# Router stage of a hybrid encoder block: GpSimd's elementwise work on VectorE, the affinities sorted in four partition groups, TensorE in program order, token-layout weights at another offset

## The chip, the core and the metric

The kernel runs on one core of a Trainium2 chip. The metric is the device time in microseconds of one execution, taken as the median of several runs. The engines named below: TensorE (PE; its weight loads are PEld), VectorE (DVE), ScalarE (ACT), GpSimd (POOL), and SyncE (SP), which issues DMAs.

## What is computed

One layer of an encoder block on 1024 tokens of width 1024, in float32: windowed attention and a gated linear attention (GLA) side by side, an output projection added to x, then an expert-choice mixture of 16 SwiGLU experts, then a gate with per-layer embeddings and a last norm. The change is in the router stage between the output projection and the experts, and in the weights of the first projections. Cut to these:

```python
a = rmsnorm(h, norm_mix[l])
proj = a @ w_in[l]            # q, k, v, q_gla, k_gla, v_gla, r_gla, z, gates
...
h = h + merged @ w_out[l]
xn = rmsnorm(h, norm_ffn[l])
aff = softmax(xn @ w_router)                          # 1024 tokens x 16 experts
top_aff, top_idx = top_k(swapaxes(aff, 1, 2), 128)    # each expert takes 128 tokens
xg = xn[top_idx]
hid = silu(xg @ w_gate) * (xg @ w_up)
y = (hid @ w_down) * top_aff                          # added back at top_idx
...
h = h + sigmoid(rmsnorm(h) @ w_pg) * (p[l] @ w_ple)
```

## The kernel before

Every float32 operand of a large product is split into a rounded upper part and a lower part that holds the rest (`split`: a cast on ScalarE, a subtraction on VectorE or on the engine named), and a product is three matmuls in a row (`mm3`, lines 109 to 111). The 1024 tokens are eight tiles of 128.

**The first projections.** `piece` (line 196) loads a column block of w_in of 8 x 128 rows and 256 columns and splits it into wh and wl. In `proj_tok` such a weight is the moving operand, 128x256, and a block of the transposed activations aT (128x128) the stationary one; the result has tokens on its partitions. This "token layout" is used for k and v (w_kv, 8 tiles x 8 blocks x 3 matmuls = 192), for q (two pieces, 384) and for GLA's v (one piece a head, 768). In `proj_T`, for the rest, the weight is stationary. Tiles come from pools whose tiles are whole lines of 128 bytes (`Lines`); those of wh and wl lie in the pool whl (4 buffers), q's second piece in wqp.

**The router stage.** The loop over tiles t calls `w_half(t, c, between)` for both halves c of the 1024 output columns: 8 blocks k of three 128x512 matmuls each into one bank, and then, on VectorE, the sum ht = 0.5 * bank + x (line 995). At the start of tile t the next tile's input is split by `msplit` (lower part on GpSimd from tile 1 on). After the second half, ScalarE squares ht and VectorE makes 1/rms of it (`rstd_of`, lines 113 to 136, some ten instructions of 128x1). The dictionary `between` says before which block k a step of the tile before is called:

- `h_turned`: eight transposes of ht into two banks "tr", copied to hT by ScalarE
- `router`: eight small matmuls of hT with the router's weights; logits copied by ScalarE
- `affinities`: a transpose back, then the softmax over 16 experts (VectorE, ScalarE) into affA
- `aff_turned`: affA of the tile transposed to 16 experts x 128 tokens, copied by ScalarE into cand; the row xa (ht times the norm's gain, on GpSimd, with affinities and 1/rms behind it) goes to DRAM for the gather

The four steps stand at k = 2, 4, 6 of half 0 and k = 2 of half 1. After tile 2 the weights w_ple are split (lower part on GpSimd); after tile 5 `p_turned` turns the embeddings p through the two banks "tr" and splits them.

**The sort.** Each expert needs its 128 largest affinities. `top128` takes eight maxima a round (MAX8) and strikes them out (MATCH_REPLACE8): on 16 partitions, 256 candidates wide, for tiles 0 and 1, 2 and 3, 4 and 5, 16 rounds each; `merge` joins two sorted lists by a bitonic net (`larger`, then seven stages of max and min). Tiles 6 and 7 are sorted at the end in halves of 64. Then the threshold cg, the masks, the positions of the chosen tokens (`tokens`) and the gather of the first expert's rows follow.

**What sets the order.** A scheduler orders each engine's instructions from the dependencies and its own estimates of time; it may put an instruction ahead of one that is written earlier. Only in the expert stage are TensorE's instructions tied to program order (`on_pe`). The product p @ w_ple (`p_product`) is written behind the gather; the scheduler puts it in the tail, between the last projection and the gather.

## Time and profile before

| | |
|---|---|
| median of 3 runs | 1739.63 us (1738.83 to 1740.87) |
| the profiled execution's own time | 1741.5 us |
| its span, first to last instruction | 1739.8 us |
| mean granted TensorE clock | 0.983 |
| busy: TensorE, VectorE, ScalarE, GpSimd | 1658.0, 1201.4, 902.2, 196.4 us |
| router stage (tile 1 to the end of the projection) | 894 to 1010 us |
| its tail (to the first expert's matmul) | 1010 to 1048 us |

The busy time of an engine is what its instructions took; a stretch's granted clock is a share of TensorE's full 2.4 GHz, and 0.5 is its other level, 1.2 GHz. Engines wait for each other by semaphores; the profile names for each wait the instruction that ended it.

### The profile page before, as it was taken

To read this page: it belongs to the slowest core of one execution; us is meant where nothing else is said; L and a number is where in the kernel's file an instruction comes from. 1 tells how busy PE (TensorE), PEld (TensorE's weight loads), DVE (VectorE), ACT (ScalarE), POOL (GpSimd) and SP (SyncE) were. 2 spreads that over 40 slices of the span, in tenths; PEclk is the share of its full clock that TensorE was granted. 3 is DMA by queue.
4 is the path that set the end of the run, shared out by engine and by line. 5 is a ranking of instruction groups with operands and counts; after the bars stand their busy time and mean duration, and the time that the engine had idled before them with its cause. 6 is when DMAs were issued, how large, how long until landed. Compare 5 with 4: busy or idle time off the path is not lost. (4 is left out here: it accounts for less than half of the span.)

```text
span 1739.8 us, 23112 instructions
## 1 busy us (share of the span) xinstructions
PE 1658.0 (95%) x8795; PEld 1361.8 (78%) x8795; DVE 1201.4 (69%) x2256; ACT 902.2 (52%) x1259; POOL 196.4 (11%) x197
## 2 busy tenths in 40 slices
PE   7998999999999999999998859999999999999897
PEld 6977766768888888988876647888888887787786
DVE  7546765543464646473367898999999998888676
ACT  4235555352444444351032236777777777777642
POOL 1013300000000000000034320111111111000010
PEclk9999999999999999999998889999999999999999
DMA  6032401415121212027442379999999999993811
GB/s 231 2 105 110 133 13 61 133 61 194 39 84 37 84 38 72 14 102 237 143 174 98 120 295 408 371 393 393 385 398 394 395 384 373 377 376 97 283 49 49
DMA packets 123607, 335.06 MB, mean 193 GB/s; under 512 B 9180, under 2 KB 41988, under 8 KB 123496
## 3 DMA queue, kind: packets, MB, share of 16 engines
q1 hardware_dynamic: 106784, 277.96, 43.6%
q0 software_dynamic: 14704, 53.17, 9.0%
q10 hardware_dynamic: 2008, 2.46, 0.4%
q8 instruction: 69, 1.13, 0.3%
q14 instruction: 42, 0.34, 0.1%
HBM read 290.50 MB, written 43.06 MB: 192 GB/s over the span
## 5 line engine op out<-in xcount | busy, mean ns | idle before, releaser
L106 DVE TENSOR_TENSOR slot<-slot 128x2048 fp32r<-128x2048 f32 (+1 forms) x193 | 438.0, 2283 | 52.7 <-ACT slot L106 50.2
L106 ACT CAST slot<-slot 128x2048 fp32r<-128x2048 f32 (+1 forms) x200 | 374.9, 1879 | 129.9 <-PE ps_mm L1195 50.8
L109 PE MATMUL ps_mm<-aT_h,wh 128*128 128x512 f32 x512 | 203.3, 397 | 1.2 <-ACT sgr L246 1.2
L111 PE MATMUL ps_mm<-aT_h,wl 128*128 128x512 f32 x512 | 204.4, 399 | 0.0
L110 PE MATMUL ps_mm<-aT_l,wh 128*128 128x512 f32 x512 | 203.9, 398 | 0.0
L109 PEld LDWEIGHTS ps_mm<-aT_h,wh 128*128 128x128 f32 x512 | 97.3, 190 | 18.8 <-ACT sgr L246 1.4
L111 PEld LDWEIGHTS ps_mm<-aT_h,wl 128*128 128x128 f32 x512 | 97.5, 190 | 18.4 <-issue 1.2
L110 PEld LDWEIGHTS ps_mm<-aT_l,wh 128*128 128x128 f32 x512 | 97.3, 190 | 18.5 <-issue 1.2
L106 DVE TENSOR_TENSOR wl<-raw,wh 128x2048 fp32r<-128x2048 f32 (+1 forms) x29 | 61.5, 2121 | 65.0 <-ACT wh L106 65.0
L1195 PE MATMUL ps_b<-slot,xt_h 128*128 128x512 f32 x256 | 100.1, 391 | 4.0 <-DVE slot L106 4.0
L1195 PE MATMUL ps_mm<-slot,xt_h 128*128 128x512 f32 x256 | 100.2, 392 | 2.7 <-DVE slot L106 2.7
L1194 PE MATMUL ps_mm<-slot,xt_h 128*128 128x512 f32 x256 | 101.5, 396 | 0.5 <-ACT xt_h L106 0.5
L1194 PE MATMUL ps_b<-slot,xt_h 128*128 128x512 f32 x256 | 101.0, 395 | 0.0
L1196 PE MATMUL ps_mm<-slot,xt_l 128*128 128x512 f32 x256 | 100.1, 391 | 0.5 <-DVE xt_l L106 0.5
L106 ACT CAST wh<-raw 128x2048 fp32r<-128x2048 f32 (+1 forms) x30 | 52.0, 1734 | 93.4 <-PE ps_mm L110 89.1
L1196 PE MATMUL ps_b<-slot,xt_l 128*128 128x512 f32 x256 | 99.8, 390 | 0.0
L109 PE MATMUL ps_mm<-wh,aT_h 128*128 128x256 f32 x320 | 91.8, 287 | 0.9 <-DVE sgr L588 0.9
L111 PE MATMUL ps_mm<-wh,aT_l 128*128 128x256 f32 x320 | 90.6, 283 | 1.5 <-DVE aT_l L106 1.5
L110 PE MATMUL ps_mm<-wl,aT_h 128*128 128x256 f32 x320 | 90.8, 284 | 0.0
L109 PE MATMUL ps_mm<-slot 128*128 128x512 f32 x192 | 79.9, 416 | 0.0
L111 PE MATMUL ps_mm<-slot 128*128 128x512 f32 x192 | 77.8, 405 | 0.0
L110 PE MATMUL ps_mm<-slot 128*128 128x512 f32 x192 | 77.6, 404 | 0.0
(392 smaller groups left out, 3893.5 us busy)
## 6 DMA issues: line engine op xcount, KB each, us to landing
slot<-in_w_exp_gate_dram SPq DMA_DIRECT2D x64, 1024.0 KB, 7.7
slot<-in_w_exp_down_dram SPq DMA_DIRECT2D x64, 1024.0 KB, 8.1
slot<-in_w_exp_up_dram SPq DMA_DIRECT2D x60, 1024.0 KB, 7.6
raw<-in_w_in_dram SPq DMA_DIRECT2D x16, 1024.0 KB, 6.5
raw<-in_w_in_dram SPq DMA_DIRECT2D x14, 512.0 KB, 5.2
sg_d<-sgr POOLq DMA_DIRECT2D x14, 512.0 KB, 3.0
xn_d<-xa POOLq DMA_DIRECT2D x8, 520.5 KB, 4.3
xt<-in_x_dram SPq DMA_DIRECT2D x8, 512.0 KB, 6.6
```

Of the source, the lines that this page charges most:

```text
L106: return nc.scalar.copy(hi, src), eng.tensor_sub(lo, src, hi)
L109: nc.tensor.matmul(out_ps, sh, mh, start=start, stop=False)
L110: nc.tensor.matmul(out_ps, sh, ml, start=False, stop=False)
L111: nc.tensor.matmul(out_ps, sl, mh, start=False, stop=stop)
L1194: on_pe(nc.tensor.matmul(po[c], src[0][:, kk], hi[:, k, cc], start=first, stop=False))
L1195: on_pe(nc.tensor.matmul(po[c], src[0][:, kk], lo[:, k, cc], start=False, stop=False))
L1196: on_pe(nc.tensor.matmul(po[c], src[1][:, kk], hi[:, k, cc], start=False, stop=last))
```

## The change

1. **Token-layout weights.** `Lines` and `pool` take `behind`: the tiles of whl and wqp become 256 bytes longer, and a tile may begin some bytes behind its line. w_kv, w_q's first piece and the heads' w_v begin 192 bytes behind, w_q's second piece 64. In the built programs these operands begin, counted in units of 256 bytes, at 128 before (w_q's second piece at 0) and at 64 afterwards, all of them; the stationary aT at 128 in both.
2. **GpSimd.** The lower parts of `msplit` and of w_ple and the product xa are made by VectorE. GpSimd keeps the two small copies into xa, its DMA issues and five memsets.
3. **The sort.** The affinities of a tile go to 16 partitions in one of four groups (from partition 0, 32, 64, 96), so that one MAX8 serves up to four lists. Tiles 0 to 3 are sorted at once behind tile 3's turn (two halves of 64, eight rounds each), 4 and 5 behind tile 5's (each in two groups of 64 candidates), 6 and 7 each alone (four groups of 32, four rounds). Lists in different groups are copied side by side (`beside`) and joined or merged. Nothing is sorted before tile 3's turn.
4. **Order.** All matmuls and transposes go through `matmul` and `turn`, and from the router loop to the end of the experts TensorE is in program order. The steps stand at other places: `h_turned` at k = 3 and `router` at k = 6 of half 0, `affinities` at k = 1 and `aff_turned` at k = 7 (k = 3 for t = 6, 7) of half 1. Behind the last tile the p product is cut in eight pieces of six matmuls, written between the last tile's steps.
5. The token numbers of all experts lie in one tile, idxs.

```diff
-    def tile(self, shape, dt, **kw):
+    def tile(self, shape, dt, behind=0, **kw):
         n = math.prod(shape[1:])
+        if self.behind:
+            at = behind // SIZE[dt]
+            t = self.pool.tile([shape[0], n + self.behind // SIZE[dt]], dt, **kw)[:, at:at + n]
+            return self.shaped(t, shape)
...
+    def on_pe(ins):
+        if in_order[0]:
+            if behind[0] is not None:
+                tc.add_manual_dep(ins.ins, behind[0].name, ..., reason="program order")
+            behind[0] = ins.ins
+        return ins
...
-    whl = ctx.enter_context(pool("whl", bufs=4))
+    TOK = 192
+    whl = ctx.enter_context(pool("whl", bufs=4, behind=256))
...
-        w_v = piece([(0, w_in[:, C_VG + h * 256:C_VG + (h + 1) * 256])])
+        w_v = piece([(0, w_in[:, C_VG + h * 256:C_VG + (h + 1) * 256])], behind=TOK)
...
+    def sorted_tiles(t):
+        c = cand[t]
+        n = 128 // cut[t]
+        if n == 128:
+            for i in range(2):
+                largest(c[:, i * 64:i * 64 + 64], part[:, i * 64:i * 64 + 64], 64)
+            return joined(b1, part[:, 0:64], part[:, 64:128], b2)
+        largest(c, part[:, 0:n], n)
+        beside(part, n, ((0, 1), (2, 3)))
+        return joined(b1[0:80, 0:2 * n], part[0:80, 0:n], other[0:80, 0:n], b2[0:80, 0:2 * n])
...
+    def four_tiles():
+        s = sorted_tiles(0)
+        beside(s, 128, ((0, 1), (2, 3)))
+        s = merged(s[0:80], other[0:80], slice(0, 80), b2)
+        beside(s, 128, ((0, 2),))
+        merged(s[0:NE], other[0:NE], slice(0, NE), top)
+
+    def two_tiles():
+        s = sorted_tiles(4)
+        beside(s, 128, ((0, 2),))
+        s = merged(s[0:NE], other[0:NE], slice(0, NE), b2)
+        merged(top[0:NE], s, slice(0, NE), top)
+
+    def one_tile(t):
+        s = sorted_tiles(t)
+        beside(s, 64, ((0, 2),))
+        return joined(cand[0][0:NE], s[0:NE, 0:64], other[0:NE, 0:64], top2[0:NE])
...
-        split(hl[:, 0], hl[:, 1], mT[t // 2][:, :, t % 2 * 128:t % 2 * 128 + 128], nc.gpsimd if t else nc.vector)
+        split(hl[:, 0], hl[:, 1], mT[t // 2][:, :, t % 2 * 128:t % 2 * 128 + 128])
...
-        nc.gpsimd.tensor_mul(xa[:, 0:D], hts[t], nffn)
+        nc.vector.tensor_mul(xa[:, 0:D], hts[t], nffn)
...
-        if t == 2:
-            top128(cand[0], top[0], 256)
-        elif t in (4, 6):
-            top128(cand[t - 2], srt, 256)
-            merge(srt)
+        if t == 3:
+            four_tiles()
+        elif t == 5:
+            two_tiles()
+        elif t == 6:
+            merged(top[0:NE], one_tile(6), slice(0, NE), top)
...
-        before = [partial(f, t - 1) for f in steps] if t else []
-        w_half(t, 0, dict(zip((2, 4, 6), before)))
-        w_half(t, 1, dict(zip((2,), before[3:])))
+        was = [{}, {}]
+        if t:
+            was = [{3: partial(h_turned, t - 1), 6: partial(router, t - 1)},
+                   {1: partial(affinities, t - 1), (3 if t > 5 else 7): partial(aff_turned, t - 1)}]
+        for c in range(2):
+            w_half(t, c, was[c])
...
+    p_half(0)
+    for f, more in ((h_turned, (1,)), (router, (2,)), (affinities, (3, 4)), (aff_turned, (5, 6, 7))):
+        f(NT - 1)
+        for n in more:
+            p_half(n)
+    last = one_tile(NT - 1)
```

What it moves, at three places. In these rows a line number is that of the kernel they are from; slot stands for several buffers, ps_mm, ps_tr, ps_a and ps_b for banks.

**VectorE at the first sort.** Before, the sort of tiles 0 and 1 is written behind tile 2's turn, but the scheduler starts it in tile 2's projection, two tiles of candidates wide, and the sum of that tile's second half (SCALAR_TENSOR_TENSOR ht<-ps_mm) stands among its first rounds:

```order
L916 MAX top_8463<-cand_8458 16x8
L918 MATCH_REPLACE cand_8458<-top_8463,cand_8458 16x256
L916 MAX top_8463<-cand_8458 16x8
L995 SCALAR_TENSOR_TENSOR ht<-ps_mm,ht 128x512
L918 MATCH_REPLACE cand_8458<-top_8463,cand_8458 16x256
L916 MAX top_8463<-cand_8458 16x8
L918 MATCH_REPLACE cand_8458<-top_8463,cand_8458 16x256
L916 MAX top_8463<-cand_8458 16x8
L120 TENSOR_SCALAR rs_v_8767<-ss 128x1
L918 MATCH_REPLACE cand_8458<-top_8463,cand_8458 16x256
```

Now the sort of four tiles starts in tile 4's second half, and the sum of that half stands behind the last of its 16 MAX, ahead of the joins:

```order
L947 MATCH_REPLACE cand_8458<-part,cand_8458 128x64 x2
L945 MAX part<-cand_8458 128x8 x2
L947 MATCH_REPLACE cand_8458<-part,cand_8458 128x64 x2
L945 MAX part<-cand_8458 128x8 x2
L1063 SCALAR_TENSOR_TENSOR ht<-ps_mm,ht 128x512
L969 TENSOR_TENSOR b_8463<-part 128x64
L970 TENSOR_TENSOR b_8463<-part 128x64
L131 TENSOR_TENSOR slot<-slot 128x1024
L959 TENSOR_TENSOR b_8464<-b_8463 128x2x32
L960 TENSOR_TENSOR b_8464<-b_8463 128x2x32
L144 TENSOR_SCALAR rs_v_9094<-ss 128x1
L1123 TENSOR_TENSOR xa<-ht,nffn 128x1024
```

The sum moved from behind the fifth of 16 rounds to behind the last of 16, and a split and xa (128x1024) stand behind it.

**TensorE around the turn of the affinities.** Before, in tile 3's loop, the turn of tile 2's affinities (16x128) stands between the three matmuls of a product:

```order
L111 MATMUL ps_mm<-slot 128x512
L109 MATMUL ps_mm<-slot 128x512
L1045 MATMUL ps_a<-ident,affA 16x128
L110 MATMUL ps_mm<-slot 128x512
L111 MATMUL ps_mm<-slot 128x512
L109 MATMUL ps_mm<-slot 128x512
L110 MATMUL ps_mm<-slot 128x512
```

Now, from tile 4's loop into tile 5's: the transposes of the logits, the turn of tile 3's affinities, and the turn of tile 4's ht:

```order
L127 MATMUL ps_a<-ident,lg_8958 128x128
L124 MATMUL ps_mm<-slot 128x512 x18
L127 MATMUL ps_a<-ident,affA 16x128
L124 MATMUL ps_mm<-slot 128x512 x12
L127 MATMUL ps_tr<-ident,ht 128x128 x8
L124 MATMUL ps_mm<-slot 128x512 x9
```

Between the turn of the affinities, which starts the sort, and the turn of ht, which needs the sum behind the sort, now stand 12 matmuls.

**TensorE in the tail.** Before, the scheduler has put the last tile's steps among the matmuls of the p product (ps_b):

```order
L1010 MATMUL ps_tr<-ident,ht 128x128 x4
L109 MATMUL ps_b<-slot 128x512
L110 MATMUL ps_b<-slot 128x512
L111 MATMUL ps_b<-slot 128x512
L1010 MATMUL ps_tr<-ident,ht 128x128 x4
L1021 MATMUL ps_a<-hT,wr 32x128 x4
L109 MATMUL ps_b<-slot 128x512
L110 MATMUL ps_b<-slot 128x512
L111 MATMUL ps_b<-slot 128x512
L109 MATMUL ps_b<-slot 128x512
L1021 MATMUL ps_a<-hT,wr 32x128 x4
L110 MATMUL ps_b<-slot 128x512
```

Now they are in the order of the program, the p product in pieces between them:

```order
L124 MATMUL ps_mm<-slot 128x512 x15
L124 MATMUL ps_b<-slot 128x512 x6
L127 MATMUL ps_tr<-ident,ht 128x128 x8
L124 MATMUL ps_b<-slot 128x512 x6
L124 MATMUL ps_a<-hT,wr 32x128 x8
L124 MATMUL ps_b<-slot 128x512 x6
L127 MATMUL ps_a<-ident,lg_9630 128x128
L124 MATMUL ps_b<-slot 128x512 x12
L127 MATMUL ps_a<-ident,affA 16x128
L124 MATMUL ps_b<-slot 128x512 x18
L127 MATMUL ps_a<-ident,cg 128x16 x2
```

The turn of the last affinities (16x128) has 30 matmuls of the p product ahead of it, and 18 behind.

## Rows read from the trace of the kernel before

**Rows 1.** The table of stretches of core 0, by stage: the router stage, its tail, and the part of the expert stage that follows. Columns: the stretch, its length, busy us (and instructions) of TensorE's matmuls, its weight loads, VectorE, ScalarE and GpSimd, the granted TensorE clock as a share of full speed, the busy share of the DMA engines, GB/s.

```profile
894.00:1010.00 116.00, 100.41 (x532) 77.24 (x530) 90.74 (x292) 28.84 (x64) 45.96 (x42) 0.91 0.34 124
1010.00:1048.00 38.00, 17.60 (x106) 12.72 (x104) 31.57 (x163) 13.64 (x20) 8.93 (x9) 0.75 0.83 318
1048.00:1435.00 387.00, 385.46 (x1861) 317.72 (x1861) 354.93 (x224) 300.53 (x233) 53.45 (x23) 1.00 1.02 391
```

**Rows 2.** The same table for the stretches of the router stage in which the clock was granted at half; columns as in rows 1.

```profile
921.40:926.30 4.90, 4.86 (x12) 3.82 (x13) 4.42 (x14) 0.26 (x1) 0.75 (x2) 0.50 0.26 109
940.00:943.40 3.40, 3.40 (x10) 2.66 (x9) 1.87 (x7) 0.00 (x0) 0.00 (x0) 0.50 0.39 157
...
970.70:974.10 3.40, 3.40 (x10) 2.64 (x9) 3.13 (x14) 0.00 (x0) 0.00 (x0) 0.50 0.38 157
...
981.00:987.80 6.80, 4.44 (x20) 2.83 (x20) 4.07 (x16) 1.17 (x2) 0.85 (x2) 0.50 0.43 151
```

**Rows 3.** The waits of TensorE from 894 to 1048 us: what it waited for and on which engine; us in total, times, the longest.

```profile
PE ps_a L1045 <- DVE affA L1039: 11.0, 6, 5.1
PE ps_a L1092 <- DVE cg L1087: 7.8, 1, 7.8
...
PE ps_tr L1010 <- DVE slot L106: 4.6, 1, 4.6
```

**Rows 4.** The timeline of VectorE while tile 2 is projected, from the 1/rms of tile 1 to the first rounds of the sort: start in us, duration in us, engine, line, operation, out<-in, shapes, and in brackets the idle time before it with what ended it.

```profile
910.77 7.80 DVE L133 SCALAR_TENSOR_TENSOR rs_y<-rs_t,rs_y 128x1 f32<-128x1 f32 x1
...
918.92 0.16 DVE L133 SCALAR_TENSOR_TENSOR rs_y<-rs_t,rs_y 128x1 f32<-128x1 f32 x1
...
922.14 0.42 DVE L916 MAX8 top<-cand 16x8 f32<-16x256 f32 x1 [0.21 <-ACT cand L1046]
...
923.10 0.42 DVE L916 MAX8 top<-cand 16x8 f32<-16x256 f32 x1
```

**Rows 5.** The timeline of GpSimd over the same stretch; columns as in rows 4.

```profile
911.66 2.38 POOL L1049 TENSOR_TENSOR xa<-ht,nffn 128x1024 f32<-128x1024 f32 x1
914.02 4.54 POOL L806 TENSOR_TENSOR slot<-slot 128x2048 fp32r<-128x2048 f32 x1
...
921.36 0.20 POOL L1050 COPY xa<-affA 128x16 f32<-128x16 f32 x1 [1.34 <-DVE affA L1039]
```

**Rows 6.** VectorE's groups of instructions from 894 to 1010 us, by shape: line, operation, out<-in, shapes, count | busy us, mean ns | idle before them.

```profile
L133 DVE SCALAR_TENSOR_TENSOR rs_y<-rs_t,rs_y 128x1 f32<-128x1 f32 x14 | 19.5, 1395 | 0.2
L916 DVE MAX8 srt<-cand 16x8 f32<-16x256 f32 x32 | 13.2, 412 | 1.4 <-ACT cand L1046 0.9
...
L916 DVE MAX8 top<-cand 16x8 f32<-16x256 f32 x16 | 6.6, 414 | 0.5 <-ACT cand L1046 0.2
```

**Rows 7.** The timeline of VectorE at the one split of 128x1024 that it makes itself (tile 0's); columns as in rows 4.

```profile
881.75 1.22 DVE L106 TENSOR_TENSOR slot<-slot 128x1024 fp32r<-128x1024 f32 x1
```

**Rows 8.** The timeline of TensorE in the projection of tile 2, five steps apart; columns as in rows 4 (the durations of matmuls overlap, so a step is read from the starts).

```profile
914.87 0.39 PE L109 MATMUL ps_mm<-slot 128*128 128x512 f32 x1
...
916.00 0.39 PE L111 MATMUL ps_mm<-slot 128*128 128x512 f32 x1
```

**Rows 9.** The timeline of VectorE in the tail, from the last sum of the projection to the first token numbers; columns as in rows 4.

```profile
1010.00 0.21 DVE L916 MAX8 hs<-cand 16x8 f32<-16x64 f32 x1
...
1010.39 0.67 DVE L995 SCALAR_TENSOR_TENSOR ht<-ps_mm,ht 128x512 f32<-128x512 f32 x1
...
1025.68 0.33 DVE L916 MAX8 hs<-cand 16x8 f32<-16x64 f32 x2
...
1026.32 0.33 DVE L916 MAX8 hs<-cand 16x8 f32<-16x64 f32 x2
...
1028.15 0.22 DVE L916 MAX8 hs<-cand 16x8 f32<-16x64 f32 x1
...
1028.71 0.22 DVE L916 MAX8 hs<-cand 16x8 f32<-16x64 f32 x1
...
1030.46 0.21 DVE L935 TENSOR_TENSOR hs<-srt 16x64 f32<-16x64 f32 x1
...
1030.85 0.21 DVE L935 TENSOR_TENSOR srt<-hs 16x64 f32<-16x64 f32 x1
...
1032.76 0.28 DVE L922 TENSOR_TENSOR gtl<-top,srt 16x128 f32<-16x128 f32 x1
...
1039.15 0.22 DVE L1127 TENSOR_SCALAR idx<-ps_a 128x1 int32<-128x1 f32 x1 [0.47 <-PE ps_a L1125]
```

**Rows 10.** The timeline of TensorE in the tail, at the turn of the last tile's affinities; columns as in rows 4.

```profile
1018.46 0.27 PE L1045 MATMUL ps_a<-ident,affA 128*16 128x128 f32 x1 [1.53 <-DVE hs L916]
```

**Rows 11.** The timeline of TensorE in the queries' projection with w_q's first piece, from the first to the 25th matmul of one unbroken chain; columns as in rows 4.

```profile
69.34 0.28 PE L109 MATMUL ps_b<-wh,aT_h 128*128 128x256 f32 x1
...
72.22 0.28 PE L109 MATMUL ps_b<-wh,aT_h 128*128 128x256 f32 x1
```

**Rows 12.** The same with w_q's second piece, from the first to the 24th.

```profile
62.64 0.28 PE L109 MATMUL ps_b<-wh,aT_h 128*128 128x256 f32 x1
...
65.37 0.28 PE L111 MATMUL ps_b<-wh,aT_l 128*128 128x256 f32 x1
```

**Rows 13.** The timeline of TensorE in a chain of the attention branch's output projection, 13 steps apart; its moving operand begins at a multiple of 256 bytes.

```profile
319.88 0.39 PE L110 MATMUL ps_mm<-atT_l,wh 128*128 128x512 f32 x1
...
322.91 0.40 PE L111 MATMUL ps_mm<-atT_h,wl 128*128 128x512 f32 x1
```

More of the change, by code (lines that the diff above doesn't have):

```diff
@@ L54, in lines @@
 @contextmanager
[L55 removed]
+def lines(pool, behind=0):
     with pool as p:
[L57 removed]
+        yield Lines(p, behind)
 @with_exitstack
@@ L74, in tile_hybrid_block, with pool @@
     out = out[0]
-    def pool(name, bufs=1, side=None, space=None):
+    def pool(name, bufs=1, side=None, space=None, behind=0):
         kw = {}
@@ L84, in pool @@
         made = tc.tile_pool(name=name, bufs=bufs, **kw)
-        return made if space is not None or name == "small" else lines(made)
+        return made if space is not None or name == "small" else lines(made, behind)
     ctx.enter_context(tc.tile_pool(name="edge", bufs=1, side="right")).tile([128, 24], F32, name="edge")
@@ L102, in bcast_row, with matmul, turn @@
         return bass.AP(tensor=ap1d.tensor, offset=ap1d.offset, ap=[[0, 128], [1, n]])
+    in_order, behind = [False], [None]
+    def on_pe(ins):
+        if in_order[0]:
+            if behind[0] is not None:
+                tc.add_manual_dep(ins.ins, behind[0].name,
+                                  mybir.DependencyInfo(mybir.DependencyClass.NoSync, mybir.DependencyReason.DATA),
+                                  reason="program order")
+            behind[0] = ins.ins
+        return ins
+    def matmul(*args, **kw):
+        return on_pe(nc.tensor.matmul(*args, **kw))
+    def turn(*args):
+        return on_pe(nc.tensor.transpose(*args))
     def split(hi, lo, src, eng=nc.vector):
@@ L191, in tile_hybrid_block, with piece @@
     posT = const.tile([128, NT, NE], BF16, name="posT")
-    whl = ctx.enter_context(pool("whl", bufs=4))
-    def piece(loads, kc=KC, n=256, hl=None, cuts=1, eng=nc.vector):
+    TOK = 192
+    whl = ctx.enter_context(pool("whl", bufs=4, behind=256))
+    def piece(loads, kc=KC, n=256, hl=None, cuts=1, eng=nc.vector, behind=0):
         raw = wraw.tile([128, kc, n], F32, tag="raw", name="raw")
-        h, l = [(hl or whl).tile([128, kc, n], F32R, tag=x if hl else "hi", name=x) for x in ("wh", "wl")]
+        h, l = [(hl or whl).tile([128, kc, n], F32R, tag=x if hl else "hi", name=x, behind=behind)
+                for x in ("wh", "wl")]
         for i in range(cuts):
@@ L938, in ordered, with joined, beside, merged @@
             s //= 2
[L939 to L946 removed]
+        return b[cur]
+    def joined(dst, a, b, free):
+        n = a.shape[-1]
+        b = b[:, ::-1]
+        nc.vector.tensor_tensor(dst[:, 0:n], a, b, op=ALU.max)
+        nc.vector.tensor_tensor(dst[:, n:2 * n], a, b, op=ALU.min)
+        return ordered([dst, free], n // 2)
+    def beside(src, n, pairs):
+        for a, b in pairs:
+            nc.vector.tensor_copy(other[a * 32:a * 32 + 16, 0:n], src[b * 32:b * 32 + 16, 0:n])
+    def sorted_tiles(t):
[8 more added lines that the diff above has]
+        return joined(b1[0:80, 0:2 * n], part[0:80, 0:n], other[0:80, 0:n], b2[0:80, 0:2 * n])
+    def merged(a, b, p, to):
+        larger(part[p], a, b)
+        return ordered([part[p], to[p]], 64)
+    def four_tiles():
[13 more added lines that the diff above has]
+        return joined(cand[0][0:NE], s[0:NE, 0:64], other[0:NE, 0:64], top2[0:NE])
+    top2 = o1.tile([128, 128], F32, name="top2")
     def msplit(t):
         hl = slot(rawB, (2, KC, 128), F32R)
[L951 removed]
+        split(hl[:, 0], hl[:, 1], mT[t // 2][:, :, t % 2 * 128:t % 2 * 128 + 128])
         return hl
@@ L1044, in aff_turned @@
         pa = bank("a")
-        nc.tensor.transpose(pa[0:NE, 0:128], aff, ident)
-        placed = nc.scalar.copy(place[t], pa[0:NE, 0:128]).ins
+        turn(pa[0:NE, 0:128], aff, ident)
+        n = 128 // cut[t]
+        for q in range(cut[t]):
+            to, by = cand[t][(group[t] + q) * 32:(group[t] + q) * 32 + NE], pa[0:NE, q * n:q * n + n]
+            if q % 2 and t == NT - 1:
+                nc.vector.tensor_copy(to, by)
+            else:
+                placed = nc.scalar.copy(to, by).ins
         xa = o2.tile([128, TW], F32, name="xa", bufs=1)
-        nc.gpsimd.tensor_mul(xa[:, 0:D], hts[t], nffn)
+        nc.vector.tensor_mul(xa[:, 0:D], hts[t], nffn)
         nc.gpsimd.tensor_copy(xa[:, D:D + NE], aff)
@@ L1117, in tile_hybrid_block @@
     st = {}
+    idxs = eg.tile([128, NE], I32, name="idxs", bufs=1)
     def tokens(e):
@@ L1158, in next_pool @@
         return cycle[(n_pieces[0] - 1) % len(cycle)]
-    behind = [None]
-    def on_pe(ins):
-        if behind[0] is not None:
-            tc.add_manual_dep(ins.ins, behind[0].name,
-                              mybir.DependencyInfo(mybir.DependencyClass.NoSync, mybir.DependencyReason.DATA),
-                              reason="program order")
-        behind[0] = ins.ins
     def turned(src, th, tl, g, tag):
```

157 lines of the change are left out of this document (72 added, 85 removed).

## The prediction

> **What bounds the kernel now.** The first view read is the table of stretches by stage [rows 1]. In the expert stretch (1048 to 1435 us) TensorE is busy 385.46 of 387 us at full clock beside a DMA share of 1.02: the change touches no instruction there. The stage that it rewrites, 894 to 1010, is different: TensorE 100.41 of 116 us, granted clock 0.91, VectorE 90.74, GpSimd 45.96, DMA only 0.34. So 15.6 us are idle TensorE in a stage whose transfers have room. The second view cuts out the stretches in which the clock was granted at 0.50, that is 1.2 GHz in place of 2.4 [rows 2]: TensorE was busy 4.86 + 3.40 + 3.40 + 4.44 = 16.1 us in them, half of which, 8.0 us, is lost. Each followed an idle stretch of TensorE. The stage has thus 23.6 us to give.
>
> TensorE's waits [rows 3] name what it waits for: affA from VectorE (11.0 us in 6 waits), p's splits (slot, 4.6 us); behind the stage, cg (7.8 us). VectorE's timeline shows why affA is late [rows 4]: a 128x1 instruction, 0.16 us when it repeats, stands 7.80 us from 910.77, while GpSimd works on xa (2.38 us) and w_ple's lower part (4.54 us) [rows 5]. Fourteen such instructions took 19.5 us [rows 6], 19.5 - 14 x 0.16 = 17.3 us too many. The longest of these waits, 5.1 us [rows 3], ends where the first stretch of half clock begins [rows 2].
>
> **GpSimd's work goes to VectorE.** Seven splits and eight xa products of 128x1024 at VectorE's 1.22 us, and w_ple's lower part, twice as long, at some 2.4 us [rows 7]: 15 x 1.22 + 2.4 = 20.7 us added, of which 17.3 come back since nothing on GpSimd holds the 128x1 instructions. What GpSimd keeps (copies of 0.2 us, DMA issues) [rows 5] costs nothing. Behind VectorE's added instructions are queued the sums ht and the 1/rms chain, and TensorE waits for those.
>
> **The sort** before has 32 + 16 rounds on 16x256 [rows 6] at 923.10 - 922.14 = 0.96 us each [rows 4], 46 us. Afterwards, within the stage: 16 rounds on 128x64 in pairs (0.64 a pair), 8 alone (0.56), 4 on 128x32 (some 0.5), all priced by the 16x64 rows [rows 9], 5.1 + 4.5 + 2.0 = 11.6 us; 62 pairs of max and min at 0.38 [rows 9], 23.6 us; five `larger` and nine copies, some 3 us. Together 38 us, so the sort is no shorter; what changes is its place. It all comes from tile 3's turn of affinities on. There VectorE has 38 us of it and per tile two sums of 0.67 [rows 9], xa and a split of 1.22, and some 3.3 us of small ones, about 23 us for what is left of the stage; 61 us, against three tiles of (100.41 - 8.0) / 7 = 13.2 us on TensorE [rows 1, 2] and the tail. So VectorE sets the pace of the last three tiles.
>
> **Stalls by place.** Tiles 1 to 4 run without a wait, since no GpSimd work is ahead of affA. In tile 5 the turn of ht's second half waits for the sum behind the 16 MAX and 14 MATCH_REPLACE of `four_tiles`: 0.6 us for the copy of the candidates, 4.8 us of rounds, 0.7 for the sum, less 12 matmuls of cover at (916.00 - 914.87) / 5 = 0.226 [rows 8] and four turns, leaves about 3.0 us. In tile 6 p's splits stand behind VectorE's merge and hold the two banks: 3.0 us by hand (4.6 us before [rows 3]). In tile 7 tile 6's affinities wait for `two_tiles`, and the turn at k = 3 leaves little cover: 2.1 us. Two of the stalls before were followed by 3.40 us at half clock, 1.7 us lost, and I take that for each [rows 2]. So 3.0 + 3.0 + 2.1 + 3 x 1.7 = 13.2 us are lost in place of 23.6: the stage gains **10.4 us**. Program order on TensorE costs nothing that I can name: the cover is counted in that order already.
>
> **The tail.** Before, it is 8.1 us from the last sum ht at 1010.39 to the turn of affA at 1018.46, 14.3 from there to the last `larger` at 1032.76, and 6.4 to idx at 1039.15 [rows 9, 10]; 28.8 us. Afterwards VectorE still owes tile 6's sort and merge when the projection ends, so the first part grows to some 11.2 us; tile 7 sorted by itself is 4 rounds of 0.5 and 13 pairs of 0.38, 7.4 us with its copies; then 6.4 again. 25.0 us, a gain of 3.8; the gather that follows meets a fuller DMA, for which I take off 1.0: **2.8 us**. The expert stretch starts earlier by the sum; its loads too, as the slots that hold them come free with the same work.
>
> **Token-layout weights.** 192 + 384 + 768 = 1344 matmuls (k and v, q, GLA's v) have these weights as the moving operand, 128x256. In the built program they began 128 bytes into a unit of 256 before (the second q piece at 0), afterwards all at 64; aT, the stationary operand, at 128 in both. The trace has the step at two of these: 24 steps of w_q's first piece take 72.22 - 69.34 = 2.88 us, 120.0 ns each [rows 11]; 23 of the second take 65.37 - 62.64 = 2.73, 118.7 ns [rows 12]. The offset does something, little; 64 is not in the trace. Bounds: half of a 512-wide step of 0.226 [rows 8] is 113 ns, a gain of 1344 x 7 = 9.4 us; a 512-wide chain whose moving operand begins at 0 steps at (322.91 - 319.88) / 13 = 233 ns against 226 [rows 13], and 7 ns lost on each would be 9.4 us slower. I take 116 ns, between 118.7 and 113: 1344 x 4 = **5.4 us**, from TensorE-bound stretches, so all of it counts.
>
> The Trainium skill speaks against this term: by "TensorE: Matmul & The Clock Gate", section "Step-by-step: what each phase is for", TensorE has "two independent SBUF read ports", and loading weights takes no bandwidth from the running matmul. By that rule where the two operands lie to each other should be worth nothing, and the sum would be 13.2 us. The trace neither settles it (120.0 against 118.7) nor shows the new offset.
>
> **The sum.** 10.4 + 2.8 + 5.4 = 18.6 us. The profiled execution took 1741.5 us (its span 1739.8), the median is 1739.6; so 1741.5 - 18.6 = 1722.9 for an execution like the profiled one, 1721 on the median's footing.
>
> **Rivals.**
> (a) The offset is worth nothing: 1739.6 - 13.2 = 1726. For it, that 118.7 and 120.0 are so near; against it, that two chains of one shape differ at all. Chance 0.27.
> (b) VectorE's pairs run denser between other work than alone: in the tail three instructions that don't wait for each other start in the 0.39 us from 1010.00 to 1010.39 [rows 9], against 0.38 for a dependent pair. If 62 pairs save 0.12 each, 7.4 us, the stalls with their half clock go: 23.6 + 2.8 = 26.4 us, 1713, and 1708 with the offset's 5.4. Chance 0.16.
> (c) The expert stretch is bound by transfers (share 1.02 [rows 1]) and its loads don't start earlier: TensorE then waits for late weights, and half of 13.2 is given back; 1733 without the offset's gain, 1728 with it. Against it, the share of 0.83 from 1010 to 1048, 6.5 us of idle transfers [rows 1]. Chance 0.13.
> (d) The new offset lengthens the step by 7 ns as in [rows 13]: 1726 + 9 = 1735. Chance 0.06.
> (e) The slower side: the trace has no MAX8 on 128 partitions. If a round there costs the 0.96 us of [rows 4] whatever its width, `four_tiles` takes 15.4 in place of 5.1 us, `two_tiles` 7.7 in place of 4.5, each `one_tile` 3.8 in place of 2.0: 17.1 us on VectorE, which sets the pace there. 13.2 - 17.1 = -3.9: 1743.5 without the offset's gain. It decides from about 0.85 us a round on. Against it, the round falls with the width from 0.96 to 0.56 [rows 4, 9]. Chance 0.06.
>
> **How the numbers follow.** The forecast has 0.32. The range from 1705 to 1735 takes in (a), (c), (d) and nearly all of (b) and leaves out (e), the offset at its best together with (b), and what I don't see: 2 in 10. A measurement of this kernel tells 0.2%, 3.5 us, from no change. Faster by more than that are the forecast, (a) to (d) nearly whole: 0.91; within it, 0.03 of (c) and (e); slower 0.06.
>
> **What would show it.** Right: no 128x1 instruction over 0.3 us on VectorE in the router stage; TensorE's waits there on ht behind the first sort, ps_tr behind p's splits, affA once, each followed by half clock; VectorE at about 9 tenths; `cg` at most 21 us behind the last projection matmul; the q chain stepping at 116 ns. Wrong: a q chain at 120 (a), a stage with under 5 us idle (b), waits for slot in the expert stretch (c), a MAX8 round near 0.96 us (e).

## The result

The changed kernel takes 1718.5 us (median of 4 runs, 1716.8 to 1719.9) against 1740.25 for the kernel before beside it: a ratio of 0.9869, 95% interval 0.9854 to 0.9884, so 20 to 25 us faster. The forecast was 1721, range 1705 to 1735. The profiled execution has a span of 1718.1 us, 21.7 less than before.

**Stages.** The table of stretches of the changed kernel; columns as in [rows 1]: the router stage (tile 1 to the end of the projection), its tail, the start of the expert stretch, the two stretches of the stage at half clock, and that of the tail.

```profile
889.00:991.00 102.00, 95.33 (x528) 74.57 (x527) 71.09 (x313) 30.15 (x69) 10.36 (x28) 0.97 0.41 153
991.00:1024.00 33.00, 16.33 (x107) 12.92 (x106) 25.15 (x110) 13.13 (x21) 6.61 (x8) 0.75 0.84 309
1024.00:1413.00 389.00, 387.45 (x1865) 319.34 (x1865) 355.56 (x224) 301.43 (x235) 53.42 (x23) 0.99 1.02 390
...
946.10:949.50 3.40, 3.40 (x11) 2.77 (x10) 3.40 (x13) 1.33 (x3) 0.51 (x1) 0.50 0.39 159
987.00:990.50 3.50, 3.50 (x10) 2.75 (x9) 2.77 (x19) 0.00 (x0) 0.00 (x0) 0.51 0.98 348
1007.50:1028.00 20.50, 7.36 (x41) 6.01 (x42) 15.00 (x29) 2.34 (x4) 5.04 (x4) 0.50 0.76 294
```

Against [rows 1] the stage is 14 us shorter and the tail 5. TensorE is idle 102.00 - 95.33 = 6.7 us in the stage, where it was 15.6, and busy 6.9 us at half clock, where it was 16.1 [rows 2]. VectorE, which took over 20.7 us of work, is busy *less*: 71.09 us, 70% of the stage, where it was 90.74. GpSimd went from 45.96 to 10.36.

**TensorE's waits** from 870 to 1028 us (what it waited for; us in total, times, longest), as in [rows 3]:

```profile
PE ps_a L127 <- DMA xg<-xn_d,idxs: 6.9, 1, 6.9
PE ps_a L127 <- DVE cg L1175: 6.1, 1, 6.1
PE ps_a L127 <- DVE affA L1107: 3.2, 2, 2.7
PE ps_tr L127 <- DVE ht L1063: 2.7, 1, 2.7
...
PE ps_tr L127 <- DVE slot L131: 0.6, 1, 0.6
```

affA fell from 11.0 to 3.2, p's splits (slot) from 4.6 to 0.6; the wait for ht, 2.7, is new.

**VectorE's groups** in the stage, as in [rows 6]:

```profile
L1063 DVE SCALAR_TENSOR_TENSOR ht<-ps_mm,ht 128x512 f32<-128x512 f32 x14 | 9.6, 688 | 19.7 <-PE ps_mm L124 19.7
...
L157 DVE SCALAR_TENSOR_TENSOR rs_y<-rs_t,rs_y 128x1 f32<-128x1 f32 x14 | 2.2, 158 | 0.4
```

The 14 instructions that took 19.5 us take 2.2. And VectorE itself waits 19.7 us for TensorE's projection (the first row's last column): it has time to spare.

**The first sort**, VectorE's timeline (columns as in [rows 4]): the first of eight interleaved double rounds, the last, the sum of tile 4's second half, the first join.

```profile
940.28 0.35 DVE L945 MAX8 part<-cand 128x8 f32<-128x64 f32 x2 [2.87 <-ACT cand L1120]
...
944.84 0.34 DVE L945 MAX8 part<-cand 128x8 f32<-128x64 f32 x2
945.10 0.67 DVE L1063 SCALAR_TENSOR_TENSOR ht<-ps_mm,ht 128x512 f32<-128x512 f32 x1
945.69 0.22 DVE L969 TENSOR_TENSOR b<-part 128x64 f32<-128x64 f32 x1
```

Eight double rounds take 945.10 - 940.28 = 4.8 us. Single rounds, 64 and 32 wide:

```profile
970.70 0.23 DVE L945 MAX8 part<-cand 128x8 f32<-128x64 f32 x1 [0.90 <-ACT cand L1120]
...
971.29 0.23 DVE L945 MAX8 part<-cand 128x8 f32<-128x64 f32 x1
...
987.12 0.19 DVE L945 MAX8 part<-cand 128x8 f32<-128x32 f32 x1
...
987.64 0.20 DVE L945 MAX8 part<-cand 128x8 f32<-128x32 f32 x1
```

0.59 and 0.52 us on 128 partitions; they were 0.56 on 16 partitions [rows 9].

**The tail**, VectorE (last sum, first MAX8 of tile 7, last `larger`, idx), then TensorE (turn of the last affinities, of the gathered rows, first expert matmul):

```profile
991.09 0.69 DVE L1063 SCALAR_TENSOR_TENSOR ht<-ps_mm,ht 128x512 f32<-128x512 f32 x1 [0.85 <-PE ps_mm L124]
...
1002.32 0.20 DVE L945 MAX8 part<-cand 128x8 f32<-128x32 f32 x1
...
1009.35 0.28 DVE L951 TENSOR_TENSOR gtl<-top,cand 16x128 f32<-16x128 f32 x1
...
1015.83 0.22 DVE L1216 TENSOR_SCALAR idxs<-ps_a 128x1 int32<-128x1 f32 x1 [0.47 <-PE ps_a L1214]
```

```profile
999.58 0.27 PE L127 MATMUL ps_a<-ident,affA 128*16 128x128 f32 x1
...
1022.68 1.94 PE L127 MATMUL ps_a<-ident,xg 128*128 128x128 f32 x8 [6.89 <-DMA xg<-xn_d,idxs]
1024.44 0.80 PE L124 MATMUL ps_mm<-slot,xt_h 128*128 128x512 f32 x1
```

From the last sum to the turn of affA 8.5 us, to the last `larger` 9.8, to idx 6.5: 24.7 in place of 28.8 [rows 9, 10]. The gather's wait is 6.9 us, 7.0 before.

**Token-layout weights**: TensorE's timeline, 24 steps of w_q's first piece:

```profile
69.71 0.28 PE L124 MATMUL ps_b<-wh,aT_h 128*128 128x256 f32 x1
...
72.43 0.28 PE L124 MATMUL ps_b<-wh,aT_h 128*128 128x256 f32 x1
```

(72.43 - 69.71) / 24 = 113.3 ns, where it was 120.0 [rows 11]. This chain is token tile 5's. The same weights in token tile 3 step at (53.68 - 50.85) / 24 = 117.9 ns:

```profile
50.85 0.28 PE L124 MATMUL ps_b<-wh,aT_h 128*128 128x256 f32 x1
...
53.68 0.28 PE L124 MATMUL ps_b<-wh,aT_h 128*128 128x256 f32 x1
```

An unbroken chain has one of these two steps: in k, v and q tiles 2 and 5 have 113.3 ns, tiles 3, 4, 6 and 7 117.8; in GLA's v, head 0 has 117.8 and heads 1 to 3 have 113.4.

**Where the 21.7 us come from**, by the starts of the same matmuls in the two traces: 5.0 us ahead when the router stage begins (first projection matmul of tile 0 at 878.1, before 883.1), 18.7 when it ends (990.7, before 1009.4), 23.4 at the first expert matmul (1024.4, before 1047.9), 22.4 at the experts' second matrix and 21.6 in the last stage. So offset 5.0, stage 13.7, tail 4.7, given back 1.8, both times where the clock was at half for longer: half clock lasts until 1028.0 here, 3.6 us into the experts (before until 1049.2, 1.3 us), and one more stretch of it, behind the experts, is 6.8 us long in place of 3.4.

### The profile page after: what moved, and what is told of

It reads as the page before. It is cut to its first block, busy times and chain, and to the rows that moved or that the text cites. A ratio compares the mean times of both kernels' runs of the same rounds, so it can differ in the third digit from the quotient of the medians.

```text
span 1718.1 us, 23091 instructions
## 1 busy us (share of the span) xinstructions
PE 1649.0 (96%) x8795; PEld 1356.6 (79%) x8795; DVE 1175.6 (68%) x2228; ACT 903.4 (53%) x1265; POOL 155.8 (9%) x186
## 5 line engine op out<-in xcount | busy, mean ns | idle before, releaser
L131 DVE TENSOR_TENSOR slot<-slot 128x2048 fp32r<-128x2048 f32 (+1 forms) x200 | 446.4, 2245 | 52.7 <-ACT slot L131 50.2
L124 PE MATMUL ps_mm<-slot,xt_h 128*128 128x512 f32 x512 | 161.6, 396 | 3.1 <-DVE slot L131 2.7
L124 PE MATMUL ps_b<-slot,xt_h 128*128 128x512 f32 x512 | 160.2, 393 | 4.0 <-DVE slot L131 4.0
L124 PE MATMUL ps_mm<-slot 128*128 128x512 f32 x576 | 142.1, 401 | 0.0
L124 PEld LDWEIGHTS ps_mm<-slot 128*128 128x128 f32 x576 | 108.1, 192 | 24.7 <-issue 1.4
L124 PEld LDWEIGHTS ps_b<-slot,xt_h 128*128 128x128 f32 x512 | 95.1, 188 | 24.8 <-DVE slot L131 5.7
L124 PEld LDWEIGHTS ps_mm<-slot,xt_h 128*128 128x128 f32 x512 | 95.7, 190 | 23.8 <-DVE slot L131 3.5
L124 PEld LDWEIGHTS ps_mm<-aT_h,wh 128*128 128x128 f32 x512 | 97.2, 190 | 18.7 <-ACT sgr L273 1.4
L124 PE MATMUL ps_mm<-slot,nT_h 128*128 128x512 f32 (+1 forms) x272 | 81.8, 381 | 0.3 <-ACT nT_h L131 0.3
```

The lines of the kernel that those rows point to most:

```text
L124: return on_pe(nc.tensor.matmul(*args, **kw))
L131: return nc.scalar.copy(hi, src), eng.tensor_sub(lo, src, hi)
```

## Experiments

For each kernel: the ratio to the kernel before with its interval, and from its trace the length of the **stage** (from the first matmul of tile 0's second half to the last projection matmul) and of the **tail** (from there to the first expert matmul). 0.001 in a ratio is 1.7 us. Kernels in different groups of runs have had different chips, so ratios are compared.

| kernel | ratio | stage | tail |
|---|---|---|---|
| before | 1 | 120.9 | 38.5 |
| the change | 0.9869 [0.9854, 0.9884] | 107.1 | 33.8 |
| e1 the offset alone | 0.9971 [0.9958, 0.9983] | 119.7 | 39.1 |
| e2 all but the offset | 0.9895 [0.9866, 0.9924] | 105.8 | 33.8 |
| e3 the move off GpSimd alone | 0.9889 [0.9861, 0.9918] | 100.6 | 39.4 |
| e4 the change, work back on GpSimd | 0.9925 [0.9896, 0.9954] | 115.6 | 36.2 |
| e5 the change, first sort behind the sum | 0.9848 [0.9831, 0.9865] | 103.5 | 34.3 |
| e6 the change, TensorE's order free | 0.9831 [0.9812, 0.9850] | 100.0 | 35.5 |
| e7 move, offset, last two tiles' sort | 0.9839 [0.9821, 0.9857] | 99.1 | 37.0 |
| e8 the change, offsets exchanged | 0.9917 [0.9899, 0.9935] | 107.1 | 33.9 |
| e9 e5 and e6 together | 0.9829 [0.9812, 0.9845] | 99.7 | 35.1 |
| e10 before, 128x1 work with one tensor | 0.9926 [0.9909, 0.9942] | 108.1 | 37.2 |
| e11 sort and places alone | 0.9962 [0.9947, 0.9978] | 113.6 | 36.2 |
| e12 e9 with other offsets | 0.9856 [0.9839, 0.9874] | 100.2 | 34.5 |

**e1, the offset alone** in the kernel before.

```diff
-    whl = ctx.enter_context(pool("whl", bufs=4))
+    whl = ctx.enter_context(pool("whl", bufs=4, behind=256))
...
-        w_v = piece([(0, w_in[:, C_VG + h * 256:C_VG + (h + 1) * 256])])
+        w_v = piece([(0, w_in[:, C_VG + h * 256:C_VG + (h + 1) * 256])], behind=TOK)
```

> The kernel before with the new offset of the token-layout weights alone (and the token numbers in one tile, which makes room for the longer weight tiles). Theory: the step of these matmuls falls from 120.0 to about 114 ns, but of the 1344 only the 768 of GLA's v stand in stretches that TensorE bounds, so 768 x 6 ns = 4.8 us: 1735.4, with the first 93 us no shorter. Rival: all 1344 count, 8 us: 1732. Rival by the rule of the two read ports: no change, 1740.

5 us, as the theory had it, and the router stage nearly unchanged. The rule of the two read ports (the Trainium skill, "TensorE: Matmul & The Clock Gate", section "Step-by-step: what each phase is for"), by which the offset would do nothing, doesn't describe this: the ratio's interval ends at 0.9983. Why 5 and not 8 was only half right. Through the k, v and q chains the trace gains 1.5 us (the 600 matmuls from the 49th to the 649th take 70.46 us in place of 71.95, in the changed kernel too), so TensorE does bound a good part of them; but of the six token tiles whose chains are unbroken only two step at 113.3 ns and four at 117.8, about 116 on average. The start of that stretch lost as much here, as it did in several kernels with and without the offset. GLA's v, with all four heads at 113.4, gains the rest.

**e2, all but the offset.**

```diff
-    whl = ctx.enter_context(pool("whl", bufs=4, behind=256))
+    whl = ctx.enter_context(pool("whl", bufs=4))
```

> The changed kernel with the token-layout weights at their old offset. Theory: the parts add up, so it loses 4.8 to 5 us against the changed kernel's 1718.5: 1723.4; step back at 119 to 120 ns, router stage and tail as in the changed kernel. Rival: part of the router stage's gain needs the other placement of the buffers, and it comes out above 1726.

0.9895 against 0.9869, 4.5 us: the parts add up within their intervals. The stage, with the same code and the same waits for ht and affA as in the changed kernel, is 105.8 us against 107.1: it has one stretch at half clock in place of two.

**e3, the move alone** in the kernel before.

```diff
-        split(hl[:, 0], hl[:, 1], mT[...], nc.gpsimd if t else nc.vector)
+        split(hl[:, 0], hl[:, 1], mT[...])
...
-        nc.gpsimd.tensor_mul(xa[:, 0:D], hts[t], nffn)
+        nc.vector.tensor_mul(xa[:, 0:D], hts[t], nffn)
```

> The kernel before with the elementwise work of GpSimd moved to VectorE, and nothing else. Theory: GpSimd's work holds VectorE's 128x1 instructions with two tensor inputs, so these fall from a mean of 1.4 to 0.16 us, 17 us come back for the 20.7 added, and the waits for affA fall from 11 us to under 5: 6 us faster, 1734, while the sort, still 256 wide, goes on holding sums. Rival: VectorE sets the pace already, and the 3.4 us more work there make it as slow as before or slower, 1740 to 1743.

Three times what I expected: 19 us, as much as e2 with the new sort, the new places and TensorE's order on top. TensorE's waits in this kernel:

```profile
PE ps_a L1092 <- DVE cg L1087: 11.2, 1, 11.2
...
PE ps_a L1045 <- DVE affA L1039: 2.5, 3, 2.0
```

The wait for p's splits is 0.3, and the stage has no stretch at half clock. Before, these two waits were 15.6 us and half clock lost 8.0: 20.8 us less, and the stage is 20.3 shorter. It is also shorter than in the changed kernel (100.6 against 107.1), with the old 256-wide sort; the tail is longer (39.4 against 33.8), with cg 11.2 us late. So the move makes the stage, the tail's gain comes from other parts of the change (which of them, this run doesn't tell), and something in the rest costs the stage 6 us.

**e4, the work back on GpSimd** in the changed kernel (e3's edit reversed).

> The changed kernel with that work back on GpSimd (lower parts of the splits and of w_ple, xa). Theory: the 128x1 instructions with two tensor inputs are held again, 15 us in all, and affA comes late in most tiles; the later places of the steps cover a part of it, so 5 to 10 us slower than 1718.5: 1726. Rival: the new places of the steps and the sort made the gain, not the move, and it stays within 3 us of 1718.5.

9.7 us slower than the change, the upper end of what was expected, and half of the 19 us that the move is worth in e3: the two kernels differ in the places of the steps, the sort and TensorE's order, and which of them covers the rest of the hold isn't told apart by this run.

**e5, the first sort behind the sum.**

```diff
-        if t == 3:
-            four_tiles()
...
+        if t == 4:
+            four_tiles()
```

The added lines stand in the loop behind tile 4's second `w_half`.

> The changed kernel with the sort of tiles 0 to 3 written behind tile 4's last sum instead of ahead of it. Theory: the 2.67 us for which the turn of ht waits behind the 16 MAX and the 1.7 us at half clock after it are owed to that order alone and go: 1714. Rival: VectorE's chain of sorts sets the pace to the end of the projection, so what is saved in tile 5 is paid at p's splits and at tile 6's affinities: 1717 to 1719.

0.9848 against 0.9869: some 3.6 us, but the intervals overlap, so the gain isn't clear of the noise. TensorE's waits:

```profile
PE ps_a L127 <- DVE affA L1107: 3.4, 3, 2.8
PE ps_tr L127 <- DVE slot L131: 2.8, 2, 2.6
```

The wait for ht, 2.7 us, is gone, but p's splits now wait 2.8 us, where they waited 0.6, and affA 3.4 for 3.2: of what is saved nearly all is paid again, as the rival had it. The stage is 3.6 us shorter all the same, because none of its stretches ran at half clock here. How much of that the edit earned is open: e2 has the changed kernel's waits and one such stretch in place of two.

**e6, TensorE free up to the experts.**

```diff
-    in_order[0] = True
     for t in range(NT):
...
     so1.close()
+    in_order[0] = True
```

> The changed kernel with TensorE left to the scheduler up to the experts, as before the change. Theory: the order on TensorE is no cause of the gain; the places of the steps are written in the program and the scheduler keeps near to them: 1718.5 within 2 us. Rival: program order is what gives affA its cover and keeps the p product between the last steps; without it the waits for affA come back, 5 us or more: over 1723.

Neither: 0.9831, 6.6 us *faster* than the change. The two intervals don't meet. Program order was the 6 us. TensorE's timeline at the first sort (turn of the affinities, the two halves of ht's turn; matmuls between them left out):

```profile
940.13 0.27 PE L127 MATMUL ps_a<-ident,affA 128*16 128x128 f32 x1
...
943.01 0.60 PE L127 MATMUL ps_tr<-ident,ht 128*128 128x128 f32 x4
...
946.29 0.66 PE L127 MATMUL ps_tr<-ident,ht 128*128 128x128 f32 x4 [0.82 <-DVE ht L1063]
```

In program order the second half of the turn stood right behind the first and waited 2.67 us for the sum. The scheduler lets the second half (four transposes) stand later, with matmuls of the next product between the halves, and 0.82 us of the wait is left. TensorE waits 2.4 us for VectorE in the stage (affA 1.6, ht 0.8), where it waited 6.5 (affA, ht, slot), and no stretch is at half clock, where 3.4 us were lost to it: 7.5 us together, and the stage is 7.1 shorter. The tail is 1.7 us longer.

**e7, three parts of the five** in the kernel before: e3's edit, e1's edit, and tiles 6 and 7 sorted by `one_tile`; no new places, no program order, tiles 0 to 5 sorted as before.

```diff
-    for t in (6, 7):
-        for i in range(2):
-            top128(cand[t][:, i * 64:i * 64 + 64], hs2[:, i * 64:i * 64 + 64], 64)
-        sorted2(srt, hs2)
+    last = one_tile(7)
```

> The kernel before with three things: GpSimd's elementwise work on VectorE, the new offset, and tiles 6 and 7 alone sorted in four partition groups; the sort of tiles 0 to 5, the places of the steps and TensorE's free order stay as before. Theory: the move alone gave the router stage its gain (100.6 us from the middle of tile 0 to the last projection matmul, against 107.1 in the changed kernel), and the sort in groups shortens the tail alone, by some 5.5 us against the kernel with the move alone; with 5 us of the offset 1713.5, ahead of the changed kernel. Rival: the two don't add, since the work of the sort that leaves the tail comes into the stage on VectorE: 1718.

0.9839, where the theory had 1713.5, 0.985. It is 5 us ahead of the change (the two intervals just overlap) and has the shortest stage of all. The tail gains 2.4 us against e3, half of what was expected.

**e8, the offsets exchanged.**

```diff
-    aT_pool = sA.enter_context(pool("aT", side="right"))
-    aT_h = aT_pool.tile([128, KC, T], F32R, name="aT_h")
+    aT_pool = sA.enter_context(pool("aT", side="right", behind=256))
+    aT_h = aT_pool.tile([128, KC, T], F32R, name="aT_h", behind=192)
...
-    TOK = 192
+    TOK = 0
```

> The changed kernel with the offsets exchanged: aT's tiles 192 bytes further, at 64 in units of 256, the token-layout weights at 128 as before, all others at 128. The token matmuls have their moving operand at 128 and the stationary one at 64, the 1536 transposed ones (512 wide) the moving one at 64 and the stationary one at 128. Theory: the step depends on how the two operands lie to each other, so the token step stays at 114 ns and the 512-wide one falls from 227 to some 221: up to 9 us faster, 1710. Rival: the moving operand's own address counts: the token step goes back to 120 ns (5 us slower) and the 512-wide one falls alike, 1714. Second rival: only the token weights gain from it and 512-wide steps stay at 227: 1723.

None of the three, and 8 us slower than the change. The 512-wide steps with aT at 64, 15 of them:

```profile
503.04 0.40 PE L124 MATMUL ps_mm<-aT_h,wh 128*128 128x512 f32 x1
...
506.54 0.39 PE L124 MATMUL ps_mm<-aT_h,wh 128*128 128x512 f32 x1
```

(506.54 - 503.04) / 15 = 233 ns, where they were 227: the same as with the moving operand at 0 [rows 13]. The 256-wide token steps average 116.5 ns, but no chain has that step. GLA's head 1, 24 steps:

```profile
510.20 0.28 PE L124 MATMUL ps_mm<-wh,aT_h 128*128 128x256 f32 x1
...
512.92 0.28 PE L124 MATMUL ps_mm<-wh,aT_h 128*128 128x256 f32 x1
```

(512.92 - 510.20) / 24 = 113.3 ns here and in head 2; heads 0 and 3 and all of k, v and q step at 117.8. These are the two steps of the changed kernel, with more chains at the longer one. So for 256 columns exchanging the operands gives the same two steps, as the theory's "how the two operands lie to each other" has it, and what fails is the theory's 512-wide half: what is best for a 256-wide moving operand is not for a 512-wide one.

**e9, e5 and e6 together.**

> The changed kernel with both: TensorE free up to the experts, and the sort of tiles 0 to 3 behind tile 4's last sum. Theory: with TensorE free, the turn of ht already moves out of the way of the late sum (0.82 us idle is left there), so the second edit adds at most that: 0.5 us or less beyond the free order alone, a ratio near 0.983 to the kernel before. Rival: the two gains add, a further 3.7 us: ratio 0.981. Second rival: the later sort makes tile 6's affinities later and costs 1 to 2 us: ratio 0.984.

0.9829 against e6's 0.9831: nothing more, as the theory had it. It is the fastest version run (1711.7), with e6 and e7 within its interval.

**e10, one tensor for each 128x1 instruction**, in the kernel before; GpSimd keeps its work.

```diff
-                eng.scalar_tensor_tensor(y, t, c, y, op0=ALU.add, op1=ALU.mult)
+                eng.tensor_scalar(y, t, c, y, op0=ALU.add, op1=ALU.mult)
...
-        nc.vector.tensor_mul(nmx, nmx, rs)
+        nc.vector.tensor_scalar(nmx, nmx, rs, None, op0=ALU.mult)
```

> The kernel before, GpSimd's work where it was, with VectorE's three kinds of 128x1 instructions that read two tensors (two in the 1/rms chain, one in the affinities) written with the second one as the scalar operand of each partition. Theory: VectorE is held by GpSimd only in an instruction that reads two tensors from SBUF; the chain isn't held any more, its 17 us go, and the waits for affA fall from 11 to under 4 us; the merge of the sort, with two tensors, is held still, and so the wait for p's splits stays: 8 to 12 us faster, ratio 0.994. Rival: any VectorE instruction is held while GpSimd runs a tensor operation, so the hold only moves to the next instruction: ratio 1.000.

12.9 us, a little more than expected and two thirds of e3, with GpSimd's load untouched. VectorE's group that took 19.5 us, and TensorE's waits:

```profile
L134 DVE TENSOR_SCALAR rs_y<-rs_t,rs_y 128x1 f32<-128x1 f32 x16 | 3.2, 199 | 0.2
```

```profile
PE ps_tr L1016 <- DVE slot L106: 5.0, 1, 5.0
PE ps_a L1051 <- DVE affA L1045: 4.1, 4, 2.3
```

0.2 us each: not held. affA's wait is 4.1 in place of 11.0 us. The wait for p's splits stays (5.0): it stands behind the sort's merge, whose instructions still read two tensors (one on 16x64 took 5.17 us). But the theory's "only in an instruction that reads two tensors" is too narrow. The scaling of affA, one tensor and a scalar of each partition, took 0.23 us in the kernel before; here it stood until GpSimd's operation ended at 918.52:

```profile
915.09 3.47 DVE L1045 TENSOR_SCALAR affA<-affA,rd 128x16 f32<-128x16 f32 x1
```

```profile
913.97 4.55 POOL L812 TENSOR_TENSOR slot<-slot 128x2048 fp32r<-128x2048 f32 x1
```

In e11 a copy of 16x64 took 2.57 us in the same way. So a part of the hold did move on, as the rival had it, and what marks the instructions with one tensor that are held isn't shown.

**e11, sort and places alone**: e6 with e4's edit and the old offset.

> The sort in four groups and the new places of the steps alone: the changed kernel with GpSimd's work back, the old offset and TensorE free up to the experts. Theory: without the move the hold stays, and the tail's 5 us are most of what is left: 6 to 8 us faster than before, ratio 0.996. Rival: the later places give affA cover for the whole hold, and these parts alone make as much as the move: 17 us, ratio 0.990.

6.6 us, as the theory had it. Without the move these parts are worth a third of it.

**e12, other offsets** for the token-layout weights, in e9 (k and v 192, q 224 and 32, the heads' v 96, 160, 192, 0).

```diff
-        w_v = piece([...], behind=TOK)
+        w_v = piece([...], behind=(224, 32, 64, 128)[h])
```

> The kernel of e9 with the token-layout weights at other offsets, in units of 256 bytes (the stationary aT at 128 in all): k and v's at 192, q's pieces at 224 and 32, GLA's v of heads 0 to 3 at 96, 160, 192 and 0. Theory: the distance between the operands counts and either side is as good, so 192 steps at 114 ns like 64, and the others lie between 114 and 120. Rival: only 64 is good, and 192 steps at 119 to 120. The time is of less interest: 768 matmuls of v at about 117 ns on average would cost 2.5 us against e9, ratio 0.9845.

Head 2's chain, at 192, 24 steps:

```profile
599.85 0.28 PE L124 MATMUL ps_mm<-wh,aT_h 128*128 128x256 f32 x1
...
602.57 0.28 PE L124 MATMUL ps_mm<-wh,aT_h 128*128 128x256 f32 x1
```

113.3 ns, like 64. Averages over all steps of a chain that follow one another: 192: 115; 160: 117; 96: 118; 32 and 0: 119; 224 and 128: 120. At 192 it is again one of two steps, 113.3 (head 2, and tiles 3 and 6 of k and v) or 117.8. Both sides of aT's 128 by 64 are good, and nothing else tried reaches 113.3. The ratio is 0.9856, 4.7 us behind e9 where 2.5 were expected, within the intervals.

## Why the prediction was right, and where not

**The hold by GpSimd** was the right cause, and it is shown. In the kernel before, the 128x1 instruction from 910.77 on ended at 918.57, and GpSimd's third tensor operation in a row at 918.56 [rows 4, 5]. The first of the three, a split:

```profile
909.31 2.39 POOL L106 TENSOR_TENSOR slot<-slot 128x1024 fp32r<-128x1024 f32 x1
```

e3 takes the work away and gains 19 us; e10 leaves it and takes the second tensor away, and gains 13. The other 6 aren't taken apart. The Trainium skill has the rule, in "SBUF — State Buffer", section "Who interferes with whom": "A DVE instruction with two SBUF inputs contends with a GpSimd instruction that reads SBUF". The trace agrees: with two tensors VectorE's instructions were held, and of those with one MAX8 ran on (0.42 us from 930.22, beside GpSimd's operation from 929.70 to 932.10), and so did e10's 128x1 ones. But two tensors are not the only case: e10's scaling of affA, with one, was held too. The trace adds that VectorE didn't get in between GpSimd's instructions, so that one small instruction waited for three.

**VectorE's balance** (20.7 us added for 17.3 back) was the wrong sum: I expected 9 tenths busy, it was 7. The hold had also stretched the sort's merge; in the kernel before, one of its instructions stood until GpSimd's operation ended at 981.67:

```profile
976.79 4.96 DVE L935 TENSOR_TENSOR top<-top 16x64 f32<-16x64 f32 x1
```

And instructions that don't depend on each other overlap: from 994.47 to 995.31 in the changed kernel VectorE did two pairs of max and min and two 128x1 instructions (0.14 and 0.26 us) in 0.84 us, where I took 0.76 for two pairs alone. From this came the step that failed: "VectorE sets the pace of the last three tiles". The stretch from the first sort to the end of the projection, columns as in [rows 1]:

```profile
940.40:990.90 50.50, 43.83 (x233) 33.70 (x232) 42.95 (x236) 13.39 (x33) 4.51 (x12) 0.93 0.49 181
```

VectorE was busy 42.95 of 50.5 us there, waited 3.8 for candidates and 3.4 for TensorE's projection, and held TensorE up at three places, not throughout. What rival (b) said of pairs is so, but it didn't take all stalls away.

**Stalls by place**: 3.0, 3.0 and 2.1 us were expected in tiles 5, 6 and 7; measured 2.7, 0.6 and 2.7. The one at p's splits was mis-sized, for the reason above. Two were followed by half clock. The stage gained 13.7 in place of 10.4. That this is near is luck in part: the move alone shortens the stage by 20.3 us (e3), twice what I gave it, and program order took some 7 of it back (e6).

**Program order**: "costs nothing that I can name" was wrong, and the change was measured with that cost in it. I had counted the cover of 12 matmuls in that order, and found the wait of 3.0 us that it leaves, but didn't ask what the scheduler would have put there. e6 shows it: 6.6 us.

**The sort**: rounds priced right (0.59 for 0.56, 0.52 for 0.5, 4.8 us for the first eight), so rival (e) falls. That the new sort, with the new places, is no gain in itself while the stage lasts is shown by e3 and e6: 100.6 us with the old sort, 100.0 with the new one. In the tail, 25.0 us were expected and 24.7 measured, by two errors that cancel: the first part is 8.5, not 11.2, and the second 9.8, not 7.4. The sort of tile 7 starts only at 1002.32. Tile 6's merge ended at 999.91, before that; what came late are tile 7's candidates. ScalarE makes its last copy of them behind its copy of a piece of the p product, for which it had waited, and VectorE waits for ScalarE:

```profile
1001.27 0.60 ACT L1042 ACTIVATE slot<-ps_b 128x512 f32<-128x512 f32 x1 [0.84 <-PE ps_b L124]
1001.89 0.17 ACT L1120 COPY cand<-ps_a 16x32 f32<-16x32 f32 x1
```

```profile
1002.10 0.18 DVE L1118 COPY cand<-ps_a 16x32 f32<-16x32 f32 x1 [1.46 <-ACT cand L1120]
```

The 1.0 taken off for a fuller DMA didn't come.

**The offset**: 5.4 expected from 1344 steps at 116 ns; the steps are 113.3 or 117.8, 115.3 on average in the changed kernel, the first 576 gained only 1.5 us, and the stretch at half clock at the start, which comes in some executions with and without the offset, took 1.3 of it in the profiled one. The size was right by compensation, and the 116 by luck: no chain has it. Rival (a) falls by e1.

**Transfers** (rival c) gave back nothing that the trace shows: the experts kept 22.4 us of lead to their end, and what was lost is half clock.

What stays open: what chooses between 113.3 and 117.8 ns at one offset (the same weights have the one in tile 5 and the other in tile 3); why 64 on either side is good for 256-wide moving operands, and not for 512-wide ones.

## What to carry to other kernels

Where a tiny VectorE instruction takes microseconds in a trace, look at what GpSimd runs at that time and at how many tensors the instruction reads: writing it with the second one as a scalar operand of each partition may give back most of it, with no work moved (13 of 19 us here), though another instruction may be held in its place, as affA's scaling was in e10. A change of several parts should be run part by part: here the three edits that took work off GpSimd made the stage, and program order took 6 us of it back unseen. An order written by hand needs the scheduler's own order beside it, at each place where an instruction can come to stand behind a late operand.
